# A hybrid scan layer on one core: the pin of the scan's bursts ends at the sixth head group, and two heads' high halves are written into value buffers

## The chip, the core and the metric

The kernel runs on one core of a Trainium2 chip. The metric is the device time of one execution in microseconds (us), the median of several runs.

## What is computed

One layer of a diffusion backbone on 128 context tokens and 1024 grid tokens, all float32, with model width 1024. The two token groups share the weights; each has its own modulation vector and start states.

```
def trunk_layer(x, mod, s_gla, s_hgrn, ...):
    shift1, scale1, gate1, shift2, scale2, gate2 = jnp.split(mod, 6, axis=-1)
    h = rmsnorm(x, norm1) * (1 + scale1) + shift1
    mix, new_gla, new_hgrn = hybrid_mixer(h, ...)      # 4 GLA heads, 4 HGRN2 heads
    x = x + gate1 * mix
    h = rmsnorm(x, norm2) * (1 + scale2) + shift2
    x = x + gate2 * conv_ffn(h, w_ffn_up, ffn_conv, b_ffn_conv, w_ffn_down, grid)

# hybrid_mixer: project h @ w_in, scan each head forward and backward with gates,
#   S_t = diag(f_t) S_{t-1} + k_t v_t^T ,  o_t = S_t^T q_t
# then rmsnorm(o) * silu(g) per head, the heads side by side ("merged"), merged @ w_out
```

`mod` is `silu(c) @ w_ada + b_ada`: the ada products below.

## The kernel before

Every float32 operand of a large product is split into a high and a low half, and a product is three matmuls (high by high, high by low, low by high). The 1152 tokens are three blocks of 384 (`BL`), worked in the order 2, 1, 0. The kernel goes through norm and modulation (to about 100 us), the projections by `w_in` with the scan of six head groups beside them (to about 633), the out-projection with what is left of the sixth group (to about 810, with the second norm and modulation), and the feed-forward part (to the end). Groups 0 and 1 hold two GLA heads each, groups 2 to 5 one HGRN2 head each.

**Two streams on TensorE.** One is the *fill*: the matmuls of the projections (L602 and L616), and, when these are done, those of the out-projection (L745; `fill_steps`). A call `stream(goal, ...)` issues fill matmuls until a count of columns is reached. The other is the scan, whose steps the main loop lays between them. For each group and each block there are eight slots. Every other slot holds a *burst* (L917 to L941): 24 small matmuls (L933) that make the scores `lv` of two levels of the scan, four bursts to a block. Between bursts VectorE updates the queries `Q` (L896) and keys `k` (L898), and ScalarE mixes them into `m` (L886), which the next burst reads; VectorE copies scores into `S` (L947). `states` steps make the chunk states: a *keys* step transposes keys (L994), ScalarE copies them to `kt` (L997), and a *product* step multiplies them with the values (L1001), with the state updates on VectorE (L1013, L1018). `outs_` steps of the group before make the outputs (L1035, L1037, L1038), normalise them (L1045, L1049), transpose them (L1085), gate them and split them in `out_second`: ScalarE writes the high half `hi` (L1093), VectorE the low half (L69), and two transfers (L1097) put them into `scr_m`, from which the out-projection reads `mh`.

**The pin.** `anchor["fill"]` is the last fill matmul recorded. At the end of every even slot the main loop sets `anchor["paced"] = anchor["fill"]` (L1235), and the next burst is issued behind that matmul (L925):

```
            last = anchor.get("paced")
            with tc.high_priority(offset=BURST_AHEAD):
```

A scheduler at build time lays out each engine's order, subject to such pins, priorities and data, so TensorE's order is fixed before the kernel runs.

**The out-projection.** `fill_steps` first closes the pool of `h1`, the projections' inputs, and gives its memory to `wo` (weights), `mh` and `mh6` (merged heads). Their loads therefore wait for the last L602. For each of the first six token tiles there are two halves of 512 columns with 21 matmuls each (seven features by three). `mh` holds two features of one block, `mh6` the seventh; the eighth, the last head's, is added later (L1386). The residual `x_sample` is loaded into a value buffer (L737).

**The pools.** `vp` holds four value buffers of tag `v` (128 x 1152 float32): the groups' values, the residual tiles, the convolution weights (L758), and, from group 2's last block on, pieces of `w_ada` (L1156) that the ada products (L1166) read, one product per even slot in groups 3 and 4. `op_` holds three buffers of tag `on`, for the normed outputs (`on`, whose buffer becomes the low half) and for `hi`.

Of the kernel before, what the change touches and what calls it, by code (L numbers as in the profile page):

```python
# [9 lines left out]
F32R = mybir.dt.float32r  # L10
# [7 lines left out]
P = 128  # L18
# [3 lines left out]
NTILE = 9  # L22
KT = 8
BL = 384
# [16 lines left out]
def flat(t):  # L41
    n = len(t.shape)
    if n == 2:
        return t
    names = " ".join("abcdef"[: n - 1])
    return t.rearrange(f"p {names} -> p ({names})")
# [3 lines left out]
def kernel(ctx: ExitStack, tc: tile.TileContext, ins, outs, stop=None):  # L50
# [3 lines left out]
    def pool(stack, name, bufs, space=None, side=None):  # L54
        kw = {} if space is None else {"space": space}
        if side is not None:
            kw["side"] = side
        return stack.enter_context(tc.tile_pool(name=name, bufs=bufs, reuse_waits="tile", **kw))
# [3 lines left out]
    anchor = {}  # L62

    def after(key):
        return tc.issue_after(anchor[key].ins) if key in anchor else nullcontext()


    def split_lo(eng, out, full, hi):
        return eng.tensor_tensor(out, full, hi.bitcast(F32), op=ALU.subtract)  # L69
# [509 lines left out]
    vp = pool(es1, "v", 4)  # L579
# [7 lines left out]
    op_ = pool(es1, "on", 3)  # L587
# [79 lines left out]
    groups = []  # L667
    for n in range(6):
        u = Group()
# [142 lines left out]
    def start_group(u):  # L812
        if u.gla:
            u.wup = wupp.tile([P, 2, P], F32, name="wup4", tag="wup")
            nc.sync.dma_start(u.wup, ins["w_gla_up_pad"][u.tau])
            src = [
                ins["state_gla"][0, 0, d, 2 * u.tau : 2 * u.tau + 2].rearrange("h k v -> (h k) v") for d in range(2)
            ]
            u.new = lambda d: new_gla[0, 0, d, 2 * u.tau : 2 * u.tau + 2].rearrange("h k v -> (h k) v")
        else:  # L820
            src = [ins["state_hgrn"][0, 0, d, u.hd] for d in range(2)]
            u.new = lambda d: new_hgrn[0, 0, d, u.hd]
        for d, st, c in ((0, u.stf, 0), (1, u.stb, 7)):
            st[c] = stp.tile([P, P], F32, name="st", tag="st")
            nc.sync.dma_start(st[c], src[d])

    def gates(u, b):

        fb = fbp.tile([P, 2, BL], F32, name="fb", tag="fb")
        k = kp.tile([P, 2, BL], F32, name="k", tag="k")  # L830
        if u.gla:
            lrs = op_.tile([P, BL], F32, name="lr", tag="on")
            nc.sync.dma_start(lrs, scr_lr[b])
            pss, bcs = [], []
            for d in range(2):
                ps = ps_o.tile([P, BL], F32, name="o", tag="o")
                mm(ps, u.wup[:, d, :], lrs, start=True, stop=True)
                bc = vcol[:, col["b_gla"] + 2 * d + u.tau : col["b_gla"] + 2 * d + u.tau + 1]
                first = nc.scalar.activation(k[:, d, :], ps, AF.Abs, bias=bc)
                pss.append(ps)  # L840
                bcs.append(bc)
            with tc.issue_after(first.ins), after("sigmoid"):
                ld = nc.scalar.preload_act_table_set("natural_log_exp_and_others")
            with tc.issue_after(ld.ins):
                for d in range(2):
                    a = k[:, d, :]
                    f = fb[:, 1 - d, :]
                    nc.scalar.activation(a, a, AF.Exp, scale=-1.0)
                    nc.scalar.activation(a, a, AF.Ln, bias=one_c[:, 0:1])
                    nc.vector.tensor_scalar(f, pss[d], bcs[d], 0.0, op0=ALU.add, op1=ALU.min)  # L850
                    nc.vector.tensor_tensor(f, f, a, op=ALU.subtract)
                    anchor["exp"] = nc.scalar.activation(f, f, AF.Exp, scale=1.0 / 16.0)
            nc.scalar.activation(k[:, 0, :], u.k[b], AF.Copy)
            nc.vector.tensor_copy(k[:, 1, :], u.k[b])
            return fb, k, u.k[b]
        for i, src in ((1, u.f[b]), (0, u.bb[b])):
            dd = 0 if i == 1 else 1
            oc = om_c[:, 4 * dd + u.hd : 4 * dd + u.hd + 1]
            lc = lb_c[:, 4 * dd + u.hd : 4 * dd + u.hd + 1]
            with after("exp"):  # L860
                nc.scalar.activation(fb[:, i, :], src, AF.Sigmoid)
                nc.scalar.activation(k[:, dd, :], src, AF.Sigmoid, scale=-1.0)
            nc.vector.tensor_scalar(fb[:, i, :], fb[:, i, :], oc, lc, op0=ALU.mult, op1=ALU.add)
            nc.vector.tensor_scalar(k[:, dd, :], k[:, dd, :], oc, None, op0=ALU.mult)
        k0 = flat(sp.tile([P, 3, P], F32, name="k0", tag="S"))
        nc.gpsimd.tensor_tensor(k0, k[:, 0, :], k[:, 1, :], op=ALU.add)
        return fb, k, k0
# [214 lines left out]
    def out_second(u, i, b, on):  # L1082
        pt = ps_o.tile([P, BL], F32, name="o", tag="o")
        for j in range(3):
            nc.tensor.transpose(pt[:, j * P : (j + 1) * P], on[:, j, :], ident)  # L1085
        rs = flat(on)
        nc.vector.tensor_tensor(rs, pt, u.g[i][b], op=ALU.mult)
        if u is groups[5]:
            nc.scalar.activation(last_head[b][:, 0, :], rs, AF.Copy)
            split_lo(nc.vector, last_head[b][:, 1, :], rs, last_head[b][:, 0, :])  # L1090
            return
        hi, lo = op_.tile([P, BL], F32R, name="hi", tag="on"), rs.bitcast(F32R)
        nc.scalar.activation(hi, rs, AF.Copy)  # L1093
        split_lo(nc.vector, lo, rs, hi)
        f = 2 * u.tau + i if u.gla else 4 + u.hd
        for j, part in enumerate((hi, lo)):
            nc.gpsimd.dma_start(scr_merged[f // 2][b][:, f % 2, j, :], part.bitcast(F32))  # L1097
        merged_done.add((f, b))
# [89 lines left out]
    def stream(goal, after):  # L1188
        nonlocal streamed
        while streamed < goal:  # L1190
            with tc.issue_after(after.ins) if after is not None else nullcontext():
                got = next(steps, None)
            if got is None:
                return
            streamed += got
# [3 lines left out]
    for n, u in enumerate(groups):  # L1199
        if not u.gla:  # L1200
            u.v = [u.vpair[u.hd % 2]]
        if n == 0:
            start_group(u)
            ready = gates(u, 2)
        for bi, b in enumerate(ORDER):
            fb, k, k0 = ready
            lv = levels(u, b, fb, k, k0)
            for slot in range(8):
                at = 8 * bi + slot
                last = anchor["mm"] = next(lv)  # L1210
                if (2, 0, 6) <= (n, bi, slot) < (5, 0, 0) and slot % 2 == 0:
                    with tc.issue_after(last.ins):
                        with tc.high_priority(offset=BURST_AHEAD):
                            ada_product()
                        ada_load(spare=(n, bi) >= (2, 2))
                with tc.issue_after(last.ins):
                    outs_.step("half", at)
                    states.step("product")
                if slot == 5 and (b > 0 or n < 5):
                    if b > 0:  # L1220
                        ready = gates(u, b - 1)
                    else:
                        start_group(groups[n + 1])
                        ready = gates(groups[n + 1], 2)
                for part in range(2):
                    with tc.issue_after(last.ins):
                        if part == 0:
                            states.step("keys")
                        outs_.step("full", at)
                        if part == 1:  # L1230
                            outs_.step("full", at)
                    goal = GOALS[n] + (GOALS[n + 1] - GOALS[n]) * (16 * bi + 2 * slot + part + 1) / 48
                    stream(goal, None if n == bi == 0 else anchor["mm"] if n == 5 else last)
                    if slot % 2 == 0 and part == 1:
                        anchor["paced"] = anchor["fill"]  # L1235
            drain(lv)
            states.drain()
            states = Steps(state_steps(u, b, k))
        outs_.drain()
        outs_ = Steps(out_steps(u))  # L1240
# [96 lines left out]
    for g in range(3):  # L1337
# [37 lines left out]
        else:  # L1375
            order = (1, 2, 0, 3, 4, 5, 6, 7)
            for fs in [(f,) for f in order[:5]] + [order[5:]]:
                if fs[-1] == 7:
                    pos["slots"] = 4
                part = [(f, w_late[f] if f in w_late else next_w(), lhs(f)) for f in fs]  # L1380
# [274 lines left out]
    u, pks = {}, {}  # L1655
# [83 lines left out]
    for c in range(NHID + 1):  # L1739
        n = c + 1 if c + 1 < NHID else None  # L1740
# [208 lines left out]
    for c in range(NHID):  # L1949
        hi, lo = next_w()  # L1950
# [91 lines left out]
```

## Time and profile before

| what | value |
|---|---|
| median of 3 runs | 1584.93 us (1584.71 to 1588.38) |
| the profiled execution | 1587.02 us, its span 1585.0 us |
| granted TensorE clock, mean | 0.98 |
| busy: PE, DVE, ACT, POOL | 1504.0, 1154.0, 787.9, 727.0 us |

A profile of one execution lists every instruction with its start and length. PE is TensorE, DVE VectorE, ACT ScalarE, POOL GpSimd, SP the engine that issues most transfers (its queue is SPq). L602 is line 602 of the kernel. A row of the timeline reads start, length, engine, line, operation, result <- operand, tile; a bracket gives the idle time just before it and what ended that. Starts of consecutive matmuls can be closer than their length, since they overlap in the pipeline; what one costs in a row of them is the distance of the starts. PEclk is the share of full speed that TensorE's clock was granted.

### The profile page before, as it was taken

Reading aid. Unit: us, or ns where it says so; the run is one execution under the profiler, and the core shown is the slowest. Engines: PE = TensorE matmul, PEld = TensorE weight load, DVE = VectorE, ACT = ScalarE, POOL = GpSimd, SP = SyncE. Lnnn points to the kernel's source line nnn. Section 1 sums busy time; section 2 is a strip of 40 time slices with the busy share of each in tenths; the row PEclk is TensorE's granted clock in tenths of the full one; section 3 lists DMA queues with packets and bytes.
Section 4 is the critical chain, followed back from the end, with each engine's and each line's share of the span. In section 5 each row is a group of like instructions: output and inputs, shape, how many; then the busy total and the mean of one; then the engine's idle time right before and its main releaser. Section 6 shows DMA issues by size and latency. Waiting matters only on the chain.

```text
span 1585.0 us, 31079 instructions
## 1 busy us (share of the span) xinstructions
PE 1504.0 (95%) x12506; PEld 1260.6 (80%) x12506; DVE 1154.0 (73%) x1724; ACT 787.9 (50%) x1521; POOL 727.0 (46%) x535
## 2 busy tenths in 40 slices
PE   7999999999999999788968999999999998999997
PEld 2699989998998988567757888888888886788886
DVE  3656566565666766455689999999999999579565
ACT  3565666455454544223564444444444443457444
POOL 1412132334233331102178999999999995100001
PEclk9999999999999999899979999999999999999999
DMA  9311112336435462745511465455645566979762
GB/s 343 105 47 46 45 52 76 95 104 214 123 122 164 133 193 69 286 143 211 197 60 48 165 179 133 117 142 133 188 115 144 162 158 195 322 231 359 247 191 114
DMA packets 164650, 244.61 MB, mean 154 GB/s; under 512 B 11124, under 2 KB 107618, under 8 KB 162586
## 3 DMA queue, kind: packets, MB, share of 16 engines
q1 hardware_dynamic: 142583, 168.54, 33.3%
q0 software_dynamic: 21312, 73.41, 15.1%
q8 instruction: 98, 1.61, 0.4%
q10 hardware_dynamic: 611, 0.68, 0.1%
q14 instruction: 46, 0.38, 0.1%
HBM read 186.95 MB, written 78.71 MB: 168 GB/s over the span
## 4 chain that ended last, share of the span: by engine, by line
PE 81%; DMA 6%; DVE 5%; ACT 3%; issue 3%; POOL 2%; SPq 0%; POOLq 0%; ACTq 0%; DVEq 0%
PE u L1493 26%; PE mm L602 15%; PE xb L1904 7%; PE yb L1904 5%; PE mm L616 5%; PE x L1698 4%; PE mm L745 3%; PE lv L933 3%; PE yb L1955 2%; PE u L1386 2%; PE x L1001 2%; DMA mh<-scr_m 1%; PE mm L505 1%; DMA raw<-in_w_in_dram 1%; DMA wa<-in_w_ada_dram 1%
## 5 line engine op out<-in xcount | busy, mean ns | idle before, releaser
L1634 DVE SCALAR_TENSOR_TENSOR acc<-u,convc,acc 128x945 f32<-128x945 f32 (+2 forms) x352 | 426.8, 1218 | 8.4 <-ACT acc L1622 1.8
L69 POOL TENSOR_TENSOR wl<-raw,wh 128x1024 fp32r<-128x1024 f32 x42 | 102.5, 2443 | 249.8 <-ACT wh L131 193.9
L602 PE MATMUL mm<-h1h,wh 128*128 128x384 f32 x528 | 185.8, 352 | 0.7 <-ACT qj L514 0.7
L602 PE MATMUL mm<-h1l,wh 128*128 128x384 f32 x528 | 179.9, 341 | 0.0
L602 PE MATMUL mm<-h1h,wl 128*128 128x384 f32 x528 | 179.7, 340 | 0.0
L896 DVE TENSOR_TENSOR Q<-Q,fb 128x384 f32<-128x384 f32 x126 | 84.7, 672 | 109.4 <-PE lv L933 107.6
L69 POOL TENSOR_TENSOR wul<-sr,wuh 128x512 fp32r<-128x512 f32 (+1 forms) x68 | 123.3, 1815 | 25.4 <-ACT wuh L1479 25.2
L886 ACT ACTIVATE m<-k 128x384 f32<-128x384 f32 x126 | 70.3, 558 | 113.0 <-PE lv L933 62.6
L69 POOL TENSOR_TENSOR wul<-ra,wuh 128x1024 fp32r<-128x1024 f32 x46 | 118.8, 2583 | 9.2 <-ACT wuh L1479 6.0
L1879 POOL TENSOR_TENSOR sq<-sq,mhalf 128x1 f32<-128x1 f32 x9 | 11.1, 1238 | 217.2 <-DVE sq L1876 217.2
L602 PEld LDWEIGHTS mm<-h1h,wh 128*128 128x128 f32 x528 | 100.2, 190 | 5.5 <-issue 3.9
L602 PEld LDWEIGHTS mm<-h1l,wh 128*128 128x128 f32 x528 | 100.1, 190 | 0.6 <-issue 0.2
L602 PEld LDWEIGHTS mm<-h1h,wl 128*128 128x128 f32 x528 | 99.9, 189 | 0.8 <-issue 0.5
L616 PE MATMUL mm<-wh,h1h 128*128 128x256 f32 x288 | 83.7, 291 | 1.3 <-ACT v L641 1.2
L131 ACT ACTIVATE wh<-raw 128x1024 fp32r<-128x1024 f32 x55 | 58.1, 1058 | 51.6 <-PE mm L602 14.4
L898 DVE TENSOR_TENSOR k<-k,fb 128x384 f32<-128x384 f32 x126 | 74.2, 589 | 11.6 <-ACT m L886 7.1
L616 PE MATMUL mm<-wh,h1l 128*128 128x256 f32 x288 | 80.4, 279 | 0.0
L616 PE MATMUL mm<-wl,h1h 128*128 128x256 f32 x288 | 80.3, 279 | 0.0
L1479 ACT ACTIVATE wuh<-ra 128x1024 fp32r<-128x1024 f32 x44 | 46.3, 1053 | 37.7 <-issue 32.1
L1663 ACT ACTIVATE u2p<-u 128x512 f32<-128x512 f32 x44 | 26.3, 597 | 74.5 <-PE u L1493 71.8
L1479 ACT ACTIVATE wuh<-sr 128x512 fp32r<-128x512 f32 (+1 forms) x66 | 50.9, 773 | 22.9 <-PE x L1698 17.1
L1730 POOL TENSOR_TENSOR acc<-acc,acc 128x1152 f32<-128x1152 f32 x22 | 59.1, 2685 | 5.2 <-DVE acc L1634 5.2
(355 smaller groups left out, 4524.3 us busy)
## 6 DMA issues: line engine op xcount, KB each, us to landing
ra<-in_w_ffn_up_dram SPq DMA_DIRECT2D x88, 256.0 KB, 3.0
raw<-in_w_in_dram SPq DMA_DIRECT2D x32, 512.0 KB, 4.6
v<-in_w_ada_dram SPq DMA_DIRECT2D x27, 512.0 KB, 4.4
scr_g<-acc POOLq DMA_DIRECT2D x22, 576.0 KB, 5.4
scr_s<-late POOLq DMA_DIRECT2D x11, 1024.0 KB, 4.3
scr_t<-in_w_ffn_down_dram POOLq DMA_DIRECT2D x16, 704.0 KB, 7.2
wa<-in_w_ada_dram SPq DMA_DIRECT2D x16, 512.0 KB, 5.4
raw<-in_w_out_dram SPq DMA_DIRECT2D x13, 512.0 KB, 3.6
```

The source lines that it names most:

```text
L69: return eng.tensor_tensor(out, full, hi.bitcast(F32), op=ALU.subtract)
L602: anchor["fill"] = mm(ps, a[:, kt, :], h[kt][b], start=(n == 0), stop=(n == 23))
L616: anchor["fill"] = mm(ps, h[kt][t // 3][:, ts_], a[:, kt % 4, :], start=(n == 0), stop=(n == 23))
L886: nc.scalar.activation(aps(t, 0, [[2 * h, NB], [h, 2], [1, h]]), aps(src, 0, [[2 * h, NB], [BL + h, 2], [1, h]]), AF.Copy)
L896: nc.vector.tensor_tensor(qm, qm, aps(ff_, 2 * h - 1, [[BL - h, 2], [2 * h, NB], [0, h]]), op=ALU.mult)
L898: nc.vector.tensor_tensor(km, km, aps(ff_, BL + 2 * h - 1, [[-(BL + h), 2], [2 * h, NB], [0, h]]), op=ALU.mult)
L1479: nc.scalar.activation(hi, raw, AF.Copy)
L1493: last = mm(dst, W[x][:, a, kt, :], HB[y][b][:, kt, :], start=(start and n == 0), stop=(stop and n == 11), skip_group_check=True,)
L1634: last = nc.vector.scalar_tensor_tensor(o, u3[:, r0 + dy : r1 + dy, c0 + dx : c1 + dx], wc(3 * (dy + 1) + dx + 1), o, op0=ALU.mult, op1=AL ...
L1698: last = mm(pk, HB[h]["p"][:, 4 * half + kt, :], aps(flat(W[x]), a * 512 + kt * P, [[(b - a) * 512, 2], [1, P]]), start=(half + kt + n == ...
L1730: last = nc.gpsimd.tensor_tensor(accg, accg, accu, op=ALU.mult)
L1904: anchor["down"] = mm(banks[i], w[a][:, ts_], w[b][:, 512:1024], start=(start and j == 0 and n == 0), stop=(j == NPAIR - 1 and n == 2), sk ...
```

## The change

The `hi` of the heads of group 2 and group 4 takes a value buffer in place of one of the three `on` buffers. At the sixth group (n = 5) the pin is dropped, and from there no new one is set.

```
@@ -1089,7 +1089,11 @@  (out_second)
-        hi, lo = op_.tile([P, BL], F32R, name="hi", tag="on"), rs.bitcast(F32R)
+        if u is groups[2] or u is groups[4]:
+            hi = flat(vp.tile([P, NTILE, P], F32R, name="hi", tag="v"))[:, 0:BL]
+        else:
+            hi = op_.tile([P, BL], F32R, name="hi", tag="on")
+        lo = rs.bitcast(F32R)
@@ -1202,6 +1206,8 @@  (main loop)
+        if n == 5:
+            anchor.pop("paced")
         for bi, b in enumerate(ORDER):
@@ -1231,7 +1237,7 @@
-                    if slot % 2 == 0 and part == 1:
+                    if n < 5 and slot % 2 == 0 and part == 1:
                         anchor["paced"] = anchor["fill"]
```

TensorE's order changes in two regions, at the start of group 3 and from the end of the fifth group's outputs to the out-projection's fourth tile or so; behind that it is the same.

The first place is the end of the projections. `m_8516` and `m_8639` are operands of the last bursts of block 2 of the sixth group, `m_8850` and `k_8651` of the first burst of block 1, `h1h` and `h1l` the halves of the projection's input. TensorE's order around the matmuls with `st` (the states, which VectorE updates) before:

```order
L933 MATMUL lv<-Q,m_8516 32x32 x12
L933 MATMUL lv<-m_8511,m_8509 32x32 x12
L994 MATMUL x<-ident,k 128x128
L1038 MATMUL o<-st,Q 128x128
L1035 MATMUL o<-v,S 128x128 x2
L1001 MATMUL x<-v,kt 128x128
L1037 MATMUL o<-st,Q 128x128
```

TensorE's order at the same place now:

```order
L933 MATMUL lv<-Q,m_8639 32x64 x12
L933 MATMUL lv<-m_8634,m_8632 32x32 x12
L994 MATMUL x<-ident,k 128x128
L1038 MATMUL o<-st,Q 128x128
L1035 MATMUL o<-v,S 128x128
L1001 MATMUL x<-v,kt 128x128
L345 MATMUL x<-ident,modr 128x128 x4
L1037 MATMUL o<-st,Q 128x128
L1038 MATMUL o<-st,Q 128x128
L1035 MATMUL o<-v,S 128x128
L933 MATMUL lv<-Q,m_8850 32x32 x12
```

The burst of `m_8516` now stands one fill step earlier; that of `m_8639`, which stood 40 rows further on, is in its place; the first burst of block 1 and the transposes of the modulation rows (L345), which stood at the end of the projections, are among the state products. The bursts of `m_8906` and `m_8991`, which stood in the out-projection, are now ahead of the last L602.

The second place is the start of the out-projection. `wh` and `wl` are the halves of the weights of features 0 to 2, `wo` those of features 3 to 6; `m_9066` belongs to the last burst of block 1, `m_9157`, `m_9213`, `m_9300` and `m_9393` to the four of block 0. TensorE's order before, from features 3 to 5 of the first tile's first half on:

```order
L745 MATMUL mm<-wo,mh 128x512 x9
L933 MATMUL lv<-Q,m_8906 32x32 x12
L933 MATMUL lv<-m_8901,m_8899 32x32 x12
L1001 MATMUL x<-v,kt 128x128
L745 MATMUL mm<-wh,mh 128x512
L745 MATMUL mm<-wl,mh 128x512
L745 MATMUL mm<-wh,mh 128x512
L745 MATMUL mm<-wo,mh 128x512 x9
L745 MATMUL mm<-wo,mh_8836 128x512 x3
```

TensorE's order there now, from behind the matmuls of features 2 and 3 on:

```order
L933 MATMUL lv<-Q,m_9213 32x32 x12
L933 MATMUL lv<-m_9208,m_9206 32x32 x12
L994 MATMUL x<-ident,k 128x128 x2
L1001 MATMUL x<-v,kt 128x128 x2
L933 MATMUL lv<-Q,m_9300 32x32 x12
L933 MATMUL lv<-m_9295,m_9293 32x32 x12
L994 MATMUL x<-ident,k 128x128 x2
L1001 MATMUL x<-v,kt 128x128 x2
L745 MATMUL mm<-wo,mh 128x512 x12
L933 MATMUL lv<-Q,m_9393 32x64 x12
L933 MATMUL lv<-m_9388,m_9386 32x32 x12
L745 MATMUL mm<-wo,mh_8836 128x512 x6
```

The bursts of block 0 with their keys and products, which stood in the second and third token tile, are now all inside the first tile. Its matmuls go by pairs of features for both halves (0 and 1, 2 and 3, 4 and 5), where before the first half ran through to feature 5.

On SP, the first residual tile (L737) and the convolution weights (L758), which stood ahead of the first `wh` load of the out-projection, now stand behind its `mh`, `wo` and `mh6` loads, and one load of `w_out` stands ahead of them.

The third place is the start of group 3. TensorE's order before, where `m_6426` belongs to the third burst of its first block:

```order
L933 MATMUL lv<-Q,m_6426 32x32 x12
L933 MATMUL lv<-m_6421,m_6419 32x32 x12
L1166 MATMUL ada<-v,cT 32x256 x4
L1085 MATMUL o<-ident,on 128x128 x3
L1001 MATMUL x<-v,kt 128x128
```

TensorE's order now, 21 rows behind that burst:

```order
L602 MATMUL mm<-h1h_380,wh 128x384
L1170 MATMUL ada<-v,cT 32x256 x4
L994 MATMUL x<-ident,k 128x128 x2
L602 MATMUL mm<-h1l_404,wh 128x384
L602 MATMUL mm<-h1h_380,wl 128x384
L1170 MATMUL ada<-v,cT 32x256 x4
L602 MATMUL mm<-h1h_383,wh 128x384
```

Two ada products (L1166, now L1170) stand here that stood behind the second and the third burst of that block; the one before them moved back by 44 rows. The loads of two pieces that follow now wait for the transfers of `hi`, whose buffers they take.

## The prediction

> **What bounds the kernel now.** I read the page first, then the span cut into stretches, then the waits, TensorE's timeline and the chain inside the one stretch that is not full.
>
> ```profile
> span 1585.0 us, 31079 instructions
> PE 81%; DMA 6%; DVE 5%; ACT 3%; issue 3%; POOL 2%; SPq 0%; POOLq 0%; ACTq 0%; DVEq 0%
> ```
>
> TensorE is the chain. So the question is where TensorE is not working, stretch by stretch (stretch, length, PE busy, then the other engines; PEclk and DMA share at the end):
>
> ```profile
> 500.00:600.00 100.00, 97.76 (x1253) 89.14 (x1252) 68.86 (x145) 52.50 (x138) 30.18 (x26) 0.98 0.50 154
> 605.00:633.00 28.00, 24.93 (x291) 23.54 (x290) 15.59 (x42) 13.57 (x49) 4.79 (x6) 0.94 0.23 72
> 633.00:655.00 22.00, 11.98 (x39) 7.66 (x38) 4.60 (x14) 4.06 (x12) 3.27 (x6) 0.84 0.94 366
> 664.00:684.00 20.00, 19.53 (x226) 15.56 (x225) 15.85 (x38) 6.78 (x18) 3.73 (x6) 1.00 0.35 111
> 900.00:1200.00 300.00, 300.00 (x1460) 247.32 (x1459) 289.18 (x304) 138.16 (x185) 288.00 (x194) 1.00 0.53 148
> ```
>
> Before 600 and after 900 TensorE has no room. From 633 to 655 it works 11.98 of 22 us, at a granted clock of 0.84, while the DMA engines are 0.94 busy: a hole set by transfers, between the last projection matmul and the out-projection. What waits there, in the stretch 600 to 700 (total, times, longest):
>
> ```profile
> DVE Q L896 <- PE lv L933: 27.8, 8, 18.3
> ACT m L886 <- PE lv L933: 27.5, 6, 16.1
> PE mm L745 <- DMA mh<-scr_m: 6.8, 5, 5.1
> ```
>
> The scan's VectorE and ScalarE stand 27 us waiting for a burst (L933), 18.3 us of it at once, while TensorE stands waiting for `mh`. The burst has its operands; only the pin behind the last fill matmul holds it. TensorE's timeline of the place (start, length, in brackets the idle time before and who ended it):
>
> ```profile
> 614.20 0.79 PE L1037 MATMUL o<-st,Q 128*128 128x128 f32 x2 [2.60 <-DVE st L1018]
> 614.78 0.64 PE L1038 MATMUL o<-st,Q 128*128 128x128 f32 x2
> 633.15 0.34 PE L602 MATMUL mm<-h1h,wl 128*128 128x384 f32 x1
> 639.99 0.71 PE L1001 MATMUL x<-v,kt 128*128 128x128 f32 x4 [3.23 <-ACT kt L997]
> 642.23 0.76 PE L745 MATMUL mm<-wh,mh 128*128 128x512 f32 x1 [0.52 <-DMA mh<-scr_m]
> 647.90 0.50 PE L745 MATMUL mm<-wh,mh 128*128 128x512 f32 x1 [0.21 <-DMA mh<-scr_m]
> 654.67 2.90 PE L745 MATMUL mm<-wo,mh 128*128 128x512 f32 x6 [5.13 <-DMA mh<-scr_m]
> 659.22 2.92 PE L745 MATMUL mm<-wo,mh 128*128 128x512 f32 x12
> 663.35 0.94 PE L745 MATMUL mm<-wo,mh 128*128 128x512 f32 x3
> ```
>
> After waits of 2.60, 3.23 and 5.13 us the matmuls run at half pace: six take 2.90 us at 654.67 and twelve 2.92 us at 659.22, so 0.43 against 0.23 us each. The hole costs twice.
>
> **The change, step by step.** Edits 2 and 3 free the twelve bursts of the sixth group from the pin. What runs in their place is the order of the changed kernel: two bursts enter the stall before 614, two more with a keys/product pair (L994, L1001) go ahead of the last projection matmul, the rest stand in the hole; none stands after the first token tile. Before, five stand after it. What those hold up on the path is in the chain and the timeline:
>
> ```profile
> 623.38 0.66 PE lv L933 x48
> 626.08 0.44 PE x L345 x4
> 631.54 0.59 PE lv L933 x47
> 637.68 16.85 DMA mh<-scr_m
> 670.44 0.66 PE lv L933 x48
> 679.15 0.45 PE x L1001 x4
> 689.85 5.49 DMA mh<-scr_m
> ```
>
> ```profile
> 682.14 0.44 PE L994 MATMUL x<-ident,k 128*128 128x128 f32 x2
> 683.05 0.71 PE L1001 MATMUL x<-v,kt 128*128 128x128 f32 x4 [0.47 <-ACT kt L997]
> 683.52 0.47 PE L745 MATMUL mm<-wh,mh 128*128 128x512 f32 x1
> 688.41 0.71 PE L1001 MATMUL x<-v,kt 128*128 128x128 f32 x4 [0.97 <-ACT kt L997]
> 692.05 0.50 PE L745 MATMUL mm<-wh,mh 128*128 128x512 f32 x1 [0.18 <-DMA mh<-scr_m]
> 695.38 1.66 PE L745 MATMUL mm<-wo,mh 128*128 128x512 f32 x6 [0.78 <-DMA mh<-scr_m]
> ```
>
> *Term 1, work taken out behind the first tile.* Five bursts at 0.59 to 0.66 (as at 631.54 and 670.44), the two with narrower tiles a little less: 3.0 us. Three pairs: 682.14 to 683.52 less the 0.47 of waiting is 0.91 for two of them, for the third, whose halves stand apart between matmuls, the 0.45 of its products and about 0.1: 2.4. Their waits: 0.47 + 0.97 = 1.44. Together 6.8 us.
>
> *Term 2, when the first tile ends.* Before: 664.1 (three matmuls from 663.35 at 0.23). After, by a walk in the new order. The last projection matmul ends near 633.2 against 633.49: the two bursts (0.66 + 0.59) and eight transposes of L345 (twice 0.44) put 2.1 us into the 2.60 us stall, and its slow matmuls (five pairs from 614.20, each some 0.2 too long, and the start of the next fill: 1.35) go; VectorE's part of those bursts delays the state update behind the stall by about 1.1; the 2.35 left pay for two bursts and a pair (2.1). The hole itself stays: the three `mh` and four `wo` loads wait for that same last matmul, and 366 GB/s is what they move at. So `mh` for features 0 and 1 lands at 642.2 as before, and with waits of over 2 us ahead its twelve matmuls run slow: to 647.7, as they do now (the next, at 647.90, waits 0.21). Then a burst 0.6 and a pair with its wait 1.4: 649.7. Twelve matmuls of features 2 and 3 at 0.23: 652.5. Burst, pair: 654.4. The next burst needs the one before it back from VectorE and ScalarE:
>
> ```profile
> 658.11 0.56 DVE L896 TENSOR_TENSOR Q<-Q,fb 128x384 f32<-128x384 f32 x1 [18.35 <-PE lv L933]
> 660.87 0.56 DVE L898 TENSOR_TENSOR k<-k,fb 128x384 f32<-128x384 f32 x1
> ```
>
> From the start of the first to the end of the second is 3.3 us, two levels, for one burst. So it can start at 653.0 + 3.3 = 656.3: a wait of 1.9 us. Burst and pair to 658.3, twelve matmuls of features 4 and 5 (landed at 654.5, no longer waited for) to 661.1, the last burst to 661.7, six matmuls to 663.1. That is 1.0 earlier than before, with all twelve bursts done.
>
> *Term 3, given back.* The second block's `mh` loads start when the third tile has read its buffers (689.85) and take 5.49 us. Before, a burst of 0.66 at 693.64 lies in that wait, beside idle 0.18 and 0.78. Without it the wait is 1.6 and the burst was free: minus 0.66. Bounds: nothing, if another wait covers it, to minus 4, if the loads come 0.6 late and the wait passes 2.6 us with the half pace behind it (2.7 us, as twelve matmuls at 642.23 lose).
>
> *Term 4, edit 1.* `hi` of heads 2 and 4 moves to value buffers. ScalarE's copies and the transfers are the same ones; the third `on` buffer is spared. But the ada pieces (L1156) use the same value buffers, and in group 3 two of their loads now wait for a `hi` transfer:
>
> ```profile
> 430.21 27.33 SPq L1156 DMA_DIRECT2D v<-in_w_ada_dram  x5
> v<-in_w_ada_dram SPq DMA_DIRECT2D x8, 512.0 KB, 4.0
> 452.33 0.54 ACT L1093 ACTIVATE hi<-on 128x384 fp32r<-128x384 f32 x1
> 459.07 0.52 ACT L1093 ACTIVATE hi<-on 128x384 fp32r<-128x384 f32 x1
> 456.53 0.62 PE L1166 MATMUL ada<-v,cT 128*32 128x256 f32 x6
> 464.80 0.66 PE L1166 MATMUL ada<-v,cT 128*32 128x256 f32 x8
> ```
>
> Five such loads leave over 27 us, so they already wait for buffers, and what SP issues next stands behind them. In the new order three products move back by 44, 59 and 25 rows; the product of 456.5 then comes at about 461 (25 rows at 0.17 to 0.2 us), together with the one before it; that of 464.8 stays. The two copies stand four and six rows earlier on ScalarE. I estimate that their transfers free the buffers at 453.5 and 457.5, so that loads of 4.0 us land at 457.5 and 461.5, three microseconds ahead of the products at 461 and 464.8. I take minus 0.5, near nothing; bounds 0 to minus 5.3 (a 2.6 us stall and 2.7 of half pace).
>
> In the sixth group the first residual tile's load and the convolution weights now leave behind the `mh` and `wo` loads, and a 512 KB weight load leaves earlier. Same bytes; at 366 GB/s 512 KB is 1.4 us, so plus or minus 1.4 on the landing of `mh`, taken as nothing. They aren't needed before the first tile's end.
>
> *Sum:* 6.8 + 1.0 - 0.66 - 0.5 = 6.6 us. The profiled run took 1587.02 us (span 1585.0 and 2.0 around it), so it would be 1580.4. That run lies 2.1 above the median of the three, so on the median 1584.93 - 6.6 = **1578.3**. What follows the out-projection is full on TensorE and VectorE and only shifts.
>
> **Does the clock forgive these waits?** Half pace after 2.60 us of idle is in the rows at 614.20 and 614.78. The Trainium skill ("TensorE: Matmul & The Clock Gate", section "HAM oscillation — how this bites in real kernels") says that only gaps over about 3.4 us bring the clock down. The 2.60 row speaks against taking that as a safe line, though its window is said to run freely.
>
> **Rivals.**
>
> *The clock stays up in the hole.* After the change no single wait there is over 2.6 us. If the granted clock stays at 1, features 0 and 1 take 2.76 rather than 5.5 us; the next features land at 647.9 and end at 650.7, the burst chain follows 1.7 earlier, the tile ends at 661.4, and the time is 1576.6. Against it: half pace after 2.60. By the skill's line above this would be the outcome. Chance 0.15.
>
> *The bursts wait in line.* They stand in TensorE's order ahead of matmuls whose data is there. If a burst's return takes 4.5 us rather than 3.3, because gates and state updates share VectorE, the wait at 654 is over 2.6 us and the eighteen matmuls behind it lose 2.7 at half pace; and if VectorE's extra work (3 us for two bursts) falls wholly before the update that ends the 614 stall, its 2.35 goes too. Gain 6.6 - 2.7 - 2.35 = 1.55: 1583.4. For it: TensorE runs strictly in this order, and 3.23 us were spent at 640 on a ScalarE copy. Chance 0.27.
>
> *Slower: ada loads in group 3.* TensorE is without a gap there, so each stall counts whole. If both late loads land 3.4 us behind TensorE, because the `hi` transfers free their buffers 6.4 us later than I estimate (at 459.9 and 463.9), each costs 3.4 and 2.7 of half pace, 12.2 in all, against 6.6 + 0.5 of gain: 5.1 slower, 1590.0. It decides at 2.6 us of stall each, where the half pace sets in; below that the two cost under 5.2 and the kernel stays ahead. Against it: the median landing of 4.0 and the copies, which end by 459.6 even where they stand now. Chance 0.05.
>
> *The bursts run no earlier*, because operands and not the pin held them: 1584.9. The 18.3 us that VectorE and ScalarE stood waiting for a burst speak against it. Chance 0.04.
>
> **How the numbers follow.** Forecast 0.49, rivals as given. A difference of 0.3% (4.75 us) is about what a measurement of this kernel can tell from no change; the border is 1580.2. Faster: the forecast in four cases of five (0.39) and the warm clock, 0.54. Same: the rest of the forecast, nearly all of the line of bursts and the ineffective pin, 0.39. Slower: the ada case and the line of bursts with two lower bounds on top, 0.07. The range takes in the warm clock with 2 us of the other terms' play below and terms 3 and 4 at most of their lower bounds above: 1574.0 to 1586.0; beyond it the ada case and some of each end.
>
> **What would show it.** Right: no wait of VectorE for L933 over 5 us after 633; TensorE's busy time from 633 to 655 up by 4 to 6 us; no L933 after 664; the last L602 within 1 us of 633. Term 3: one or two waits for `mh` near 685 of 1.6 us in all. Term 4: no wait at the ada products between 440 and 480. Wrong: a wait for `m` or `Q` by L933 of over 2.6 us with half pace behind it, or a later L602.

## The result

The changed kernel takes 1575.24 us (median of 6 runs, 1569.76 to 1578.19) beside 1585.32 us of the kernel before: a ratio of 0.9928 (95% interval 0.9908 to 0.9949). Two later series of the same kernel gave 0.9946 (0.9928 to 0.9965) and 0.9922 (0.9900 to 0.9944). It is faster by 8.6 to 12.4 us, where 6.6 were forecast; by the first ratio the time is 1573.5 on the scale of the runs shown first (1584.93 x 0.9928), half a microsecond below the forecast range, in which the median itself, 1575.24, still lies.

The profiled execution took 1575.30 us. Its page and its stretches, columns as before (stretch, length, PE busy, PEld, DVE, ACT, POOL, PEclk, DMA share, GB/s):

```profile
span 1573.2 us, 31068 instructions
PE 82%; DVE 6%; DMA 5%; ACT 3%; issue 3%; POOL 2%; SPq 0%; POOLq 0%; ACTq 0%; DVEq 0%
```

```profile
605.00:633.00 28.00, 26.94 (x394) 24.22 (x393) 22.76 (x66) 19.23 (x64) 7.01 (x10) 1.00 0.29 91
633.00:655.00 22.00, 15.93 (x244) 11.40 (x242) 11.74 (x32) 8.75 (x21) 2.07 (x3) 0.84 0.99 390
```

Before the last projection matmul TensorE's 24.93 us of work became 26.94, at a clock of 1.00 in place of 0.94; in the hole 11.98 became 15.93, with VectorE at 11.74 in place of 4.60. Waits in the stretch 600 to 700:

```profile
DVE Q L896 <- PE lv L933: 11.5, 7, 6.0
PE mm L745 <- DMA mh<-scr_m: 3.8, 2, 2.2
```

VectorE's wait for bursts fell from 27.8 to 11.5 us, its longest from 18.3 to 6.0. TensorE's timeline at the same places:

```profile
611.77 0.66 PE L345 MATMUL x<-ident,modr 128*128 128x128 f32 x4 [0.50 <-ACT st L1010]
612.74 0.49 PE L1037 MATMUL o<-st,Q 128*128 128x128 f32 x2 [0.30 <-DVE st L1018]
631.83 0.34 PE L602 MATMUL mm<-h1h,wl 128*128 128x384 f32 x1
640.24 0.77 PE L745 MATMUL mm<-wh,mh 128*128 128x512 f32 x1 [2.19 <-DMA mh<-scr_m]
647.74 0.71 PE L1001 MATMUL x<-v,kt 128*128 128x128 f32 x4 [0.89 <-ACT kt L997]
653.12 0.71 PE L1001 MATMUL x<-v,kt 128*128 128x128 f32 x4 [0.97 <-ACT kt L997]
656.35 2.99 PE L745 MATMUL mm<-wo,mh 128*128 128x512 f32 x12
659.27 0.54 PE L933 MATMUL lv<-Q,m 128*32 128x64 f32 x24
661.62 0.49 PE L1035 MATMUL o<-v,S 128*128 128x128 f32 x2
683.49 0.47 PE L745 MATMUL mm<-wh,mh 128*128 128x512 f32 x1 [1.59 <-DMA mh<-scr_m]
722.32 0.71 PE L1379 MATMUL u<-wh,mh 128*128 128x512 f32 x2 [0.54 <-DVE ev L750]
```

The stall of 2.60 us is now two pieces of 0.50 and 0.30; the wait of 5.13 us for the third `mh` is gone; the last burst stands at 659, where before it stood at 694. The first product behind the out-projection fill (L1373, now L1379) starts at 722.32 where it started at 734.07:

```profile
734.07 0.70 PE L1373 MATMUL u<-wh,mh 128*128 128x512 f32 x2 [0.50 <-DVE ev L750]
```

From three marks (the last L602, the end of the first tile, that product) the difference of the two profiles splits:

| stretch | before | changed, three profiles | forecast change | measured change |
|---|---|---|---|---|
| last L602 to end of first tile | 31.0 | 29.8, 29.8, 31.3 | -0.7 | -0.7 in the mean |
| end of first tile to L1373 | 69.9 | 60.7, 61.0, 60.7 | -6.2 | -9.1 |
| L1373 to the first feed-forward matmul | 76.2 | 76.2, 75.9, 75.5 | 0 | -0.3 |

The middle line holds nearly all of the gain, and nearly all of the error. For the stretch ahead of the table, up to the last L602, 0.3 us less were forecast. The last L602 starts at 633.15 before and at 631.83, 630.40 and 629.23 in the three profiles of the changed kernel, but most of that arises ahead of 605 us and differs from execution to execution (the last section has a likely reason): a kernel that is the same up to there had it at 636.96. From 605.80 to the last L602 it was 27.35 us before, and 27.1 in the changed kernel from the same place in its order (604.69).

### The profile page after: what moved, and what is told of

The parts are those of the page before. It is cut to its first block, busy times and chain, and to the rows that moved or that the text cites. A ratio compares the mean times of both kernels' runs of the same rounds, so it can differ in the third digit from the quotient of the medians.

```text
span 1573.2 us, 31068 instructions
## 1 busy us (share of the span) xinstructions
PE 1500.9 (95%) x12506; PEld 1258.8 (80%) x12506; DVE 1153.2 (73%) x1724; ACT 788.5 (50%) x1521; POOL 726.3 (46%) x535
## 4 chain that ended last, share of the span: by engine, by line
PE 82%; DVE 6%; DMA 5%; ACT 3%; issue 3%; POOL 2%; SPq 0%; POOLq 0%; ACTq 0%; DVEq 0%
PE u L1499 26%; PE mm L602 15%; PE xb L1910 7%; PE yb L1910 6%; PE mm L616 5%; PE x L1704 4%; PE mm L745 4%; PE lv L933 3%; PE yb L1961 2%; PE u L1392 2%; PE x L1001 1%; PE mm L505 1%; DMA raw<-in_w_in_dram 1%; DMA wa<-in_w_ada_dram 1%; PE ada L1170 1%
## 5 line engine op out<-in xcount | busy, mean ns | idle before, releaser
L602 PE MATMUL mm<-h1h,wh 128*128 128x384 f32 x528 | 184.9, 350 | 0.7 <-ACT qj L514 0.7
L602 PE MATMUL mm<-h1h,wl 128*128 128x384 f32 x528 | 179.1, 339 | 0.0
L602 PE MATMUL mm<-h1l,wh 128*128 128x384 f32 x528 | 179.1, 339 | 0.0
L602 PEld LDWEIGHTS mm<-h1h,wh 128*128 128x128 f32 x528 | 99.5, 188 | 5.6 <-issue 3.9
L602 PEld LDWEIGHTS mm<-h1l,wh 128*128 128x128 f32 x528 | 99.5, 188 | 0.6 <-issue 0.2
L602 PEld LDWEIGHTS mm<-h1h,wl 128*128 128x128 f32 x528 | 99.3, 188 | 0.8 <-issue 0.5
L1485 ACT ACTIVATE wuh<-sr 128x512 fp32r<-128x512 f32 (+1 forms) x66 | 50.9, 773 | 22.9 <-PE x L1704 17.0
```

The source lines that it names most:

```text
L602: anchor["fill"] = mm(ps, a[:, kt, :], h[kt][b], start=(n == 0), stop=(n == 23))
L1485: nc.scalar.activation(hi, raw, AF.Copy)
```

## The experiments

**Which edit.** Two kernels have one part of the change each.

```
e1_pace, f2_pace:  edits 2 and 3 only; hi = op_.tile([P, BL], F32R, name="hi", tag="on")
e2_hi:             edit 1 only
```

> Only edits 2 and 3 (the pin ends at the sixth group); the high halves of groups 2 and 4 stay in the on buffers. Theory A (the whole gain is the bursts leaving the out-projection for the stall at 611 us and the hole at 633 to 655 us): 9 to 12 us below before, the changed kernel's time within 2 us. Rival B (moving the residual and convolution loads behind the mh and wo loads, which edit 1 does, is worth a good part): no more than 8 us below before. Rival C (the order of the second norm and modulation, which comes out otherwise with one edit alone, decides): off the changed kernel by 3 us or more in the stretch from 722 to 810 us, either way, with the first tile and the end of the out-projection as in the changed kernel.

> Only edit 1 (the high halves of groups 2 and 4 in value buffers); the pin stays. Theory A: within 2 us of before, with the bursts where they were and a hole as before. Rival B: 2 to 5 us below before, with mh landing 1 to 2 us earlier in the hole. Rival C: a difference of 3 us or more that lies behind the out-projection. Ada stall (the slower rival of the prediction): a wait at the ada products between 455 and 470 us.

Edits 2 and 3 alone: 1572.11 us, ratio 0.9919 (0.9902 to 0.9935). Edit 1 alone: 1583.51 us, 0.9992 (0.9981 to 1.0003). The end of the pin is the change; the value buffers are worth nothing that can be measured. In the profile of edit 1 alone the hole is as before, though the residual load, which left at 628.11 before, now leaves behind the loads of `mh`, at 640.51:

```profile
640.58 0.77 PE L745 MATMUL mm<-wh,mh 128*128 128x512 f32 x1 [4.70 <-DMA mh<-scr_m]
652.10 2.93 PE L745 MATMUL mm<-wo,mh 128*128 128x512 f32 x6 [4.46 <-DMA mh<-scr_m]
```

Two more kernels put one of the two heads into value buffers, with the pin ended as in the change.

```
e3_hi4:  if u is groups[4]:
e4_hi2:  if u is groups[2]:
```

> The change without group 2's high halves in value buffers (group 4's alone). Nothing moves in group 3 then. Theory A: within 2 us of the changed kernel. If the moved ada products of group 3 cost or give something, it is the difference to the changed kernel between 430 and 480 us; I expect less than 0.5 us there. Rival B: as the changed kernel, since the loads move with group 4's halves. Rival C: 3 us or more behind the out-projection.

> The change without group 4's high halves in value buffers (group 2's alone); the residual and convolution loads stay early, as before. Theory A: within 2 us of the changed kernel. Rival B: 2 to 4 us slower than the changed kernel, with mh landing later in the hole. Rival C: as the changed kernel, whose order behind the out-projection it nearly has.

1573.37 us (0.9922, 0.9907 to 0.9938) and 1572.31 us (0.9925, 0.9908 to 0.9941): neither the moved ada products nor the moved residual loads show in the time, and neither does the order of the second norm, which differs between these kernels. The changed kernel was then run again, and once more on one chip with edits 2 and 3 alone.

> The changed kernel as it is, a second time, to see how far its runs spread and what of its profile repeats. Theory A: 10 to 13 us below before. If the spread (1569.8 to 1578.2 us) comes from the granted clock after waits near 2 us (rival C' of the clock: the same wait is followed by half pace in one execution and not in another), its profile may show the first twelve out-projection matmuls in 2.8 us rather than 5.4.

> The changed kernel beside edits 2 and 3 alone on the same chip. If edit 1 costs nothing, the two agree within 1.5 us and both lie 9 to 12 us below before; if moving the ada products and the residual loads costs something, the changed kernel is 2 to 3 us slower than the other.

> Edits 2 and 3 alone, a second time, beside the changed kernel on the same chip. If edit 1 costs nothing: within 1.5 us of the changed kernel. If it costs: 2 to 3 us faster, and the profile shows the difference between 430 and 520 us or in the out-projection.

The series a1 gave 1574.95 us, 0.9946; f1 and f2, side by side, 1572.92 us (0.9922, 0.9900 to 0.9944) and 1572.65 us (0.9918, 0.9897 to 0.9938). Edit 1 costs nothing that these runs can tell.

**What a burst in the hole costs.** The pin comes back for the last block.

```
-                    if n < 5 and slot % 2 == 0 and part == 1:
+                    if (n < 5 or bi == 2) and slot % 2 == 0 and part == 1:
```

> The change with the pin set again in the sixth group's last block (block 0): its last three bursts and two keys/product pairs go back behind the first token tile; everything ahead of them stays as in the changed kernel. Account 1 (these bursts stand in a hole that the third mh load ends near 653 us, so they cost the first tile what they save later beyond that): the first tile ends 2.5 to 4 us earlier than in the changed kernel, the five tiles behind it take 5 to 7 us longer, 2 to 3.5 us slower in all. Account 2 (in the hole they are free): 5.5 to 7 us slower. Account 3 (packing them is a loss): as fast as the changed kernel or faster.

1577.57 us (0.9956, 0.9943 to 0.9969), 2.6 above the changed kernel beside it (a1: 0.9946, 0.9928 to 0.9965). The two intervals overlap, so the account rests on the timeline:

```profile
636.96 0.34 PE L602 MATMUL mm<-h1h,wl 128*128 128x384 f32 x1
658.58 5.93 PE L745 MATMUL mm<-wo,mh 128*128 128x512 f32 x18 [3.28 <-DMA mh<-scr_m]
664.61 0.50 PE L745 MATMUL mm<-wh,mh 128*128 128x512 f32 x1
730.32 0.70 PE L1379 MATMUL u<-wh,mh 128*128 128x512 f32 x2 [0.59 <-DMA wh<-scr_wo]
```

The first tile ends 27.7 us behind the last L602 (29.8 in the changed kernel), with a wait of 3.28 us for the third `mh` in place of the bursts, and the rest takes 65.7 us (60.7 to 61.0). From the last L602 to the first product it is 93.4 us, against 90.5 to 92.0 in the three profiles of the changed kernel. Account 1 fits: three bursts and two pairs cost 2.1 us in the hole (by the first two profiles) and 4.9 behind it, both a little under its ranges, and so they are neither free in the hole (account 2) nor a loss (account 3).

**What lies behind the excess.** The forecast charged a burst from its first row to the next engine row, 0.66 us. The rows around the burst at 670.37 of the kernel before show two matmuls beside it that take longer too:

```profile
670.05 0.39 PE L745 MATMUL mm<-wh,mh 128*128 128x512 f32 x1
670.37 0.54 PE L933 MATMUL lv<-Q,m 128*32 128x64 f32 x24
670.73 0.37 PE L933 MATMUL lv<-m,m 128*32 128x32 f32 x24
671.03 0.50 PE L745 MATMUL mm<-wh,mh 128*128 128x512 f32 x1
671.37 0.40 PE L745 MATMUL mm<-wl,mh 128*128 128x512 f32 x1
```

From 670.05 to 671.37 are 1.32 us for two matmuls of 0.23 and the burst: 0.86 for the burst. I read this as a price of each interruption and tested it with the smallest one: eight small matmuls whose result the next matmul clears, spread over eight places or all in one.

```
+                    if t >= 2:                      (e10_break1: t == 3 and half == 0, eight times)
+                        mm(ps[:, 0:P], ident, ident, start=True, stop=True)
```

> The changed kernel with eight additional 128x128 matmuls of the identity with itself, one ahead of each half of the third to the sixth out-projection tile, into a bank that the next matmul clears (they add nothing to the output). Break theory (each interruption of the stream of 512-wide matmuls costs about 0.2 us beyond the work put in): from the row before the small matmul to the second row behind it each place takes about 0.3 us more than two rows of 0.23. Rival (only the work counts, about 0.11 us a matmul): 0.1 us more at each place.

> The same eight small matmuls all in one place, ahead of the first half of the fourth tile. Break theory: eight times 0.11 us and once about 0.2: 1.1 us at that place, against 2.4 us over the eight places of the kernel with one in each. Rival: 0.9 us in both.

One place of the first kernel, then the one of the second:

```profile
674.76 0.38 PE L744 MATMUL mm<-ident 128*128 128x128 f32 x2
674.90 0.48 PE L748 MATMUL mm<-wh,mh 128*128 128x512 f32 x1
675.21 0.40 PE L748 MATMUL mm<-wl,mh 128*128 128x512 f32 x1
```

```profile
680.95 1.97 PE L744 MATMUL mm<-ident 128*128 128x128 f32 x16
682.69 0.50 PE L748 MATMUL mm<-wh,mh 128*128 128x512 f32 x1
683.02 0.39 PE L748 MATMUL mm<-wl,mh 128*128 128x512 f32 x1
```

Each float32 matmul stands as two rows. Spread: 675.21 - 674.76 - 0.23 = 0.22 us a place. In one: 683.02 - 680.95 - 0.23 = 1.84, or 0.23 each. The break theory falls: eight interruptions cost no more than one. Its rival had the price of one too low by half (0.1 expected), but was right that the price doesn't depend on how they are spread. The 0.86 of a burst is thus its cost at that place, neighbours included, and no surcharge for interrupting; for bursts themselves this wasn't tried.

**The clock in the hole.** Ten matmuls ahead of the first real one, in a bank that it clears:

```
+                    if t == 0 and half == 0:
+                        for _ in range(10):
+                            mm(ps, ws[0][0][:, 0:P], ws[0][0][:, cs], start=True, stop=True)
```

> The changed kernel with ten additional matmuls of the first weights with themselves into the first out-projection bank ahead of its real first matmul, which clears it (they add nothing to the output). Clock theory (half pace follows from the idle before mh): the first twelve out-projection matmuls take 2.8 rather than 5.4 us; at most 2 us gain, since the next mh lands near 646. Rival (half pace is due to the transfers beside it, not to the idle): they stay at 5.4 us and the kernel is 0 to 2.5 us slower.

The twelve matmuls of features 0 and 1 then run from 640.91 to 643.76, 2.85 us where the changed kernel took 5.4 in its first profile (640.24 to 645.63) and 4.5 in its second:

```profile
635.51 2.84 PE L744 MATMUL mm<-wh 128*128 128x512 f32 x10
640.91 0.50 PE L748 MATMUL mm<-wh,mh 128*128 128x512 f32 x1 [1.45 <-DMA mh<-scr_m]
643.76 0.60 PE L1004 MATMUL x<-v,kt 128*128 128x128 f32 x4
647.57 0.47 PE L748 MATMUL mm<-wh,mh 128*128 128x512 f32 x1 [0.76 <-DMA mh<-scr_m]
```

The DMA engines were as busy beside these twelve as in the changed kernel's first profile (a share of 1.03 in both), while the granted clock was 1.00 in place of 0.50, so the slow pace belongs to the idle time and not to the transfers. The other profiles agree. Only the kernel with `mh` ahead of a whole weight (below), where the twelve start without a wait, has them at full pace too, in 2.84 us. In all the others they take 4.3 to 5.7: behind waits of 1.50 to 4.70 us, and in the kernel before behind one of 0.52 with 3.23 and 0.54 just ahead of it. The next `mh` then sets the pace (0.76). 1573.73 us, 0.9935 (0.9915 to 0.9955): not to be told from the changed kernel's 0.9946 beside it.

**The order of the loads, and one group earlier.** These try for more.

```
e8_pop4:        anchor.pop("paced") at n == 4, no pin from there on; hi in the on buffers
e11_mh0first:   mh 0 ahead of the low half of the third w_out weight
e13_mh0pin:     mh 0 ahead of both halves, edits 2 and 3 alone
-        ws = list(next_ws(3))
+        ws = list(next_ws(2))
         ...
         ms = [load_merged(0, 0)]
+        ws += next_ws(1)
```

> Edits 2 and 3 one group earlier (the pin ends at the fifth group; no high half in a value buffer). TensorE has no idle time in the fifth group's stretch (97.8 of 100 us), so no burst can win there: within 2 us of the kernel with edits 2 and 3 alone (e1_pace). Rival: bursts ahead of time run into each other's VectorE work and TensorE waits in the stretch 500 to 600: 2 to 6 us slower than that.

> The changed kernel with the first mh load ahead of the low half of the third out-projection weight (512 KB) in SP's queue. Theory D (at the start of the hole TensorE waits for the first mh alone, in the order of the queue, at 366 to 390 GB/s): the first out-projection matmul starts 1.3 us earlier behind the last projection matmul (7.0 rather than 8.3 us), its wait of about 2 us shrinks by as much, the time falls by 1 to 2 us. Rival (the transfers run side by side, so the order in the queue does not matter): no change within 0.4 us.

> Edits 2 and 3 alone, with the first mh load ahead of both halves of the third out-projection weight (1 MB). Theory D: the first out-projection matmul starts 2.6 us earlier (5.7 us behind the last projection matmul), at full pace where the clock has not fallen, and the kernel is 1.5 to 3.5 us faster than with edits 2 and 3 alone, about 1569 to 1571 us. Rival (queue order does not matter), or the third mh load near 21.5 us behind the last projection matmul decides: no change.

One group earlier: 1572.86 us, 0.9930 (0.9915 to 0.9946), no difference, as expected. With the load ahead of half a weight: 1573.03 us, 0.9927 (0.9906 to 0.9947); the first out-projection matmul starts 7.3 us behind the last L602 in place of 8.1 to 8.4, and its wait stays (2.23), as a product step now stands behind it. Ahead of the whole weight, with two rows of SP's queue first:

```profile
628.83 0.46 SPq L702 DMA_DIRECT2D mh<-scr_m  x1
633.53 0.33 SPq L146 DMA_DIRECT2D wh<-scr_wo  x1
633.33 0.34 PE L602 MATMUL mm<-h1h,wl 128*128 128x384 f32 x1
636.85 0.48 PE L748 MATMUL mm<-wh,mh 128*128 128x512 f32 x1
642.55 0.46 PE L936 MATMUL lv<-Q,m 128*32 128x32 f32 x24 [1.29 <-ACT m L889]
646.30 0.80 PE L748 MATMUL mm<-wh,mh 128*128 128x512 f32 x1
```

The first matmul starts 3.5 us behind the last L602, with no wait, where 5.7 were expected. The reason is more than the order in which transfers share the engines: the first `mh` load leaves at 628.83, 4.5 us ahead of the last L602. So that load does not need the end of the projections, though the description of the kernel and the prediction say that it does. In the other kernels it stands in SP's queue behind the `wh` load (L146), which does wait for it (633.53 here), and is held with it. But the gain is lost again. A burst waits for its operand (1.29), a product for `kt` (another 1.29), the second `mh` lands at 646.26, and features 2 and 3, which read it, run at half pace from 646.30. The third `mh` lands at 653.1, ahead of its first matmul at 654.95, and no longer decides. From the last L602 to the first product behind the out-projection it is 88.0 us, against 89.3 and 89.2 in the two profiles of edits 2 and 3 alone. 1573.21 us, 0.9925 (0.9905 to 0.9946): the expected 1.5 to 3.5 us did not come in the time. No version was clearly better than the changed kernel; edits 2 and 3 alone do the same with less.

## Why the prediction was right in its mechanism and short in its size

**The mechanism** stands: the pin held the bursts, and without it they run in the stall and in the hole, as edits 2 and 3 alone show. Edit 1 was put at nothing plus a 0.5 us allowance for the ada loads; it is nothing.

**Term 2** (the first tile) came out well, in part by luck. The walk gave 30.2 us from the start of the last L602 to the end of the first tile; 29.8, 29.8 and 31.3 were measured. Two errors offset each other: the first `mh` came about 1 us sooner than walked, and from there to the end of the tile it took 21.4 to 22.9 us where the walk has 20.9. Its premise, that all `mh` loads wait for the last projection matmul, was wrong for the first, as the kernel with that load ahead of the whole weight shows. Its inner steps: the first `mh` 9.3 us behind the last L602 (8.2 to 8.4 measured), the half pace of features 0 and 1 (there in all three, 4.5 to 5.4 us for the twelve), a wait of 1.9 us ahead of the third burst (it became waits of 0.97 for `kt` and none for the burst itself, since the burst came back from VectorE in 2.7 us rather than 3.3: 651.15 to 653.87), and features 4 and 5 no longer waiting for `mh`.

**Term 3** was right: 1.59 us of waiting for the second block's `mh` in place of 0.18 + 0.78, 0.63 given back where 0.66 were forecast.

**Term 1 is the step that failed, in its size.** It had 6.8 us for the work taken out behind the first tile, net 6.2 with term 3; 9.1 were measured. Two things were missing, which together make nearly all of the 2.9 us; each place below is read to about 0.1 us:

- *A place with waits at the end, about 1.7 us.* The kernel before waits 0.36, 0.35 and 0.47 us, 1.2 in all, between transposes of the convolution weights and a keys/product pair; they were quoted nowhere and booked at nothing. From the matmul ahead (704.99) to the next one behind (707.86) are 2.87 us, some 2.65 more than one matmul needs. In the changed kernel the transposes (L764) stand apart in the fill, at 0.1 us each, and the pair's halves have matmuls between them and cost 0.3 and 0.5: 1.0 us. One wait of 0.53 at a later pair is left, as before.

```profile
704.99 0.39 PE L745 MATMUL mm<-wh,mh 128*128 128x512 f32 x1
705.22 0.25 PE L764 MATMUL x<-ident,v 99*128 99x99 f32 x1
705.82 0.31 PE L764 MATMUL x<-ident,v 99*128 99x99 f32 x1 [0.36 <-DVE convc L765]
706.49 0.44 PE L994 MATMUL x<-ident,k 128*128 128x128 f32 x2 [0.35 <-DVE convc L765]
707.40 0.71 PE L1001 MATMUL x<-v,kt 128*128 128x128 f32 x4 [0.47 <-ACT kt L997]
707.86 2.99 PE L745 MATMUL mm<-wo,mh 128*128 128x512 f32 x12
```

```profile
692.10 0.38 PE L994 MATMUL x<-ident,k 128*128 128x128 f32 x2
693.71 0.60 PE L1001 MATMUL x<-v,kt 128*128 128x128 f32 x4
699.85 0.71 PE L1001 MATMUL x<-v,kt 128*128 128x128 f32 x4 [0.53 <-ACT kt L997]
```

That the end of the pin brought this, and not another rule of the scheduler, is shown by the kernel with the pin back for the last block: there the waits of 0.35 and 0.47 us are back, though not the 0.36.

- *Bursts and pairs charged too low, about 1.2 us.* Read by the distance of the neighbours' starts, as with the 0.86 above, the six places where the five bursts and three pairs stood come to 0.86, 0.96, 0.4, 2.1, 2.6 and 1.05 us (the last without its 0.78 of waiting for `mh` and 0.1 for a transpose). That is 8.0 us, their waits for `kt` included, where 6.8 were charged. Most is missing where a burst stands without a whole pair (0.2 to 0.4), little beside a pair (0.1).

**The rivals.** *The bursts wait in line* did not happen: no wait for a burst's operand over 2.6 us. *The clock stays up in the hole* was right about the size of the loss (the kernel with ten more matmuls shows it) but in the changed kernel the clock fell: no single wait was over 2.6 us, but half pace came after less than that (last section). *Ada loads* did not stall in group 3. Of the signs, no L933 stands after 664, and the `mh` wait near 683 is 1.59 us; but VectorE still waited once for 6.0 us for a burst, at 646, behind the slow matmuls of features 0 and 1, and the last L602 came 1.3 to 3.9 us early, mostly for the reason ahead of 605 us given above. The range ended at 1574.0 because all its margin below went to the clock, and none to term 1, whose price was taken from rows as if it were exact.

## What to carry to other kernels

Where one engine waits for a transfer and another waits for work that a pacing rule holds back, end the rule at that stage: what counts is what the moved work cost where it stood. Charge work between long matmuls by the distance of the neighbours' starts, less their own pace, and put the waits that stand near it into the sum, since they move with it. A load that is waited for belongs at the head of its queue, ahead of loads that wait for something it doesn't need itself, but the gain ends at the next thing that is waited for, here a burst's operand and the second load.

## What the runs showed of the hardware

The same wait is followed by half pace in one execution and not in another. In group 4 an ada product waits for its load in every profile. In the changed kernel (1.60 us), in its second series (1.53) and in the kernel with group 4's halves alone (1.46), the row and 4 us behind it:

```profile
489.21 1.04 PE L1170 MATMUL ada<-v,cT 128*32 128x256 f32 x8 [1.60 <-DMA v<-in_w_ada_dram]
490.00:494.00 4.00, 4.00 (x27) 3.83 (x24) 1.85 (x4) 0.96 (x3) 1.09 (x2) 0.66 0.61 197
```

```profile
487.51 0.64 PE L1170 MATMUL ada<-v,cT 128*32 128x256 f32 x8 [1.53 <-DMA v<-in_w_ada_dram]
488.00:492.00 4.00, 4.00 (x24) 3.92 (x21) 2.22 (x4) 1.38 (x3) 1.46 (x2) 0.57 0.70 217
```

```profile
487.45 0.64 PE L1170 MATMUL ada<-v,cT 128*32 128x256 f32 x8 [1.46 <-DMA v<-in_w_ada_dram]
488.00:492.00 4.00, 4.00 (x38) 3.98 (x35) 2.23 (x4) 1.76 (x5) 1.48 (x2) 1.00 0.69 219
```

The clock was granted at 0.66, 0.57 and 1.00. Counted over the sixteen profiles of this study, from 130 us to the stall at 614: behind 40 waits of 1.0 to 1.49 us the clock stayed at 1.00 each time, behind 26 waits from 1.50 us on it fell to 0.50 to 0.70 in 12 (from 1.53 us) and stayed in 14 (up to 2.72 us). So in this stretch a wait can cost twice from about 1.5 us on, and what decides can't be seen in the rows. In the hole it goes one way: all 13 profiles with a wait of 1.50 us or more for the first `mh` have half pace behind it, throughout or in part. There other waits stand close by (1.03 and 0.47 us within 4 us in the changed kernel), so the length of one wait may not be all that counts; how idle time adds up was not tested.

The Trainium skill ("TensorE: Matmul & The Clock Gate", section "HAM oscillation — how this bites in real kernels") gives gaps over about 3.4 us as the rule; the waits counted here bring the clock down well below that. The Trainium skill says on the same page ("Part 1: The HAM clock gate (the "warmup" mystery)") that the window in which activity is measured runs freely. That would explain why the same wait goes both ways; no run here shows the window.

A fall like these takes about 4 us at six tenths, so some 1.6 us by estimate. The runs of both kernels spread by up to 9.5 us (1582.32 to 1591.77 for the kernel before in one series). These falls are a likely cause: in the first series of the changed kernel the fastest run (1569.76 us) has a mean granted clock of 0.986 and the slowest (1578.19) 0.982, and in each of the 17 series of four runs and more the clock tends to be lower where the time is longer (correlation -0.39 to -0.97). Which run had which fall can't be seen without its profile, so this is not shown.
